# A row-sum kernel whose first load shrinks to 128 neighbouring rows, with a block transpose and two more stores

One core of one Trainium2 chip. The metric is the time of one execution on the device, in microseconds (us), as the median of several runs. All runs quoted are at a granted clock of 1.0. A profiled run has a span of its own, from the first to the last instruction; it is 1.7 to 1.8 us shorter than the time.

## The reference

```python
x = np.random.randn(32, 512, 1024).astype(np.float32)      # 67.11 MB
def reference(x):
    return np.sum(x, axis=-1).astype(np.float32)           # 16384 sums
```

Each of 16384 rows of 4 KB is summed. Nothing is used twice, so the kernel is a stream of loads with sums beside it.

## The kernel before

The rows are taken in 8 groups. In a group each of the 128 partitions holds 16 rows that lie behind one another in memory (64 KB). Three buffers of one group each rotate. The first group comes in two loads, 4 rows and 12 rows a partition; the last group in small pieces, so that little is left to sum after the last byte. Loads are issued from the queue of SyncE (SP). `hold(a, b, why)` lets instruction a wait for b. The start barrier, where the engines wait for each other, stands ahead of the kernel's body; the first load is moved ahead of it.

```python
def issue_first_load_at_entry(nc):          # run on the finished program
    ...                                     # (finds SP's first load in its block: `load`)
        entry = list(main.instructions)
        k = next(k for k, i in enumerate(entry) if isinstance(i, mybir.InstDrain) and i.engine == SP)
        main.instructions = entry[:k] + [load] + entry[k:]     # ahead of the start barrier
...
    x_g = x.flatten_outer_dims().rearrange("(g p j) d -> g p j d", p=P, j=BIG)   # BIG = 16
    def rows_from(j, n):
        return x_g[j // BIG, :, j % BIG : j % BIG + n, :]
    FIRST = 4
...
        for g in range(last):
            t = inpool.tile([P, BIG * dim + 4], fp32)
            if g == 0:
                rows(t, 0, FIRST, 0, 0)            # load on SP, then one reduce on VectorE
                first = sums_of[-1]
                rows(t, FIRST, BIG - FIRST, FIRST, 0)
                continue
            load = rows(t, 0, BIG, g * BIG, BIG // 2 if g == last - 1 else 0)
            if g == 1:
                hold(load, first, "no descriptors of later loads while the first ones start")
...                                                # last group in five pieces
        hold(store(nc.scalar, 0, last), two, "its packets come behind those of the loads")
...
        store(nc.sync, last, last + 1)
```

Of the kernel before, what the change touches and what calls it, by code (L numbers as in the profile page):

```python
# [89 lines left out]
@with_exitstack  # L90
def kernel(
    ctx: ExitStack,
    tc: tile.TileContext,
    x: bass.AP,
    out: bass.AP,
):
    nc = tc.nc
    nc.at_finalize(issue_first_load_at_entry)
    nc.at_finalize(order_waits)
    nc.at_finalize(wait_for_the_store_at_the_clear)  # L100
    fp32 = mybir.dt.float32
    P = 128
    batch, seq, dim = x.shape
    rows = batch * seq
    J = rows // P
    BIG = 16


    x_g = x.flatten_outer_dims().rearrange("(g p j) d -> g p j d", p=P, j=BIG)
    out_v = out.rearrange("b s -> (b s)").rearrange("(g p j) -> p g j", p=P, j=BIG)  # L110

    def rows_from(j, n):
        return x_g[j // BIG, :, j % BIG : j % BIG + n, :]



    last = J // BIG - 1
    FIRST = 4
    pieces = (560, 464)

    with (
        tc.tile_pool(name="in", bufs=3) as inpool,
        tc.tile_pool(name="unread", bufs=4, space=bass.MemoryType.PSUM) as upool,
        tc.tile_pool(name="stage", bufs=1) as stpool,
        tc.manual_schedule(),
    ):
        sums = stpool.tile([P, J], fp32)

        def vec(dst, src):
            return nc.vector.tensor_reduce(  # L130
                out=dst, in_=src, axis=mybir.AxisListType.X, op=mybir.AluOpType.add
            )

        def hold(inst, until, reason):
            tc.add_manual_dep(
                inst.ins,
                until.ins.name,
                mybir.DependencyInfo(mybir.DependencyClass.Sync, mybir.DependencyReason.DATA),
                reason=reason,
            )  # L140

        def halves(dst, src):
            n = src.shape[-1] // 2
            return nc.vector.tensor_tensor_reduce(  # L144
                out=src[:, :n],
                in0=src[:, :n],
                in1=src[:, n:],
                scale=1.0,
                scalar=0.0,
                op0=mybir.AluOpType.add,  # L150
                op1=mybir.AluOpType.add,
                accum_out=dst,
            )

        def act(dst, src, n):
            unread = upool.tile([P, dim], fp32)
            nc.scalar.activation(  # L157
                out=unread[:, :n],
                in_=src,
                func=mybir.ActivationFunctionType.Copy,  # L160
                accum_out=dst,
            )

        sums_of = []

        def rows(t, a, n, j, n_act, pairs=False):
            nv = n - n_act
            block = t[:, a * dim : (a + n) * dim].rearrange("p (n d) -> p n d", d=dim)
            load = nc.sync.dma_start(out=block, in_=rows_from(j, n))  # L169
            if pairs:  # L170
                for q in range(nv):
                    sums_of.append(halves(sums[:, j + q : j + q + 1], block[:, q, :]))
            else:
                sums_of.append(vec(sums[:, j : j + nv], block[:, :nv, :]))
            for q in range(nv, n):
                act(sums[:, j + q : j + q + 1], block[:, q, :], dim)
            return load

        def store(eng, g0, g1):
            return eng.dma_start(  # L180
                out=out_v[:, g0:g1],
                in_=sums[:, g0 * BIG : g1 * BIG].rearrange("p (g j) -> p g j", j=BIG),
            )

        for g in range(last):
            t = inpool.tile([P, BIG * dim + 4], fp32)
            if g == 0:
                rows(t, 0, FIRST, 0, 0)
                first = sums_of[-1]
                rows(t, FIRST, BIG - FIRST, FIRST, 0)  # L190
                continue
            load = rows(t, 0, BIG, g * BIG, BIG // 2 if g == last - 1 else 0)
# [4 lines that stand above are left out]
        j = last * BIG  # L197
        rows(t, 0, 8, j, 4)
        rows(t, 8, 5, j + 8, 2, pairs=True)
        two = rows(t, 13, 2, j + 13, 1, pairs=True)  # L200
        a = BIG - 1



        j += a
        c, width = pieces
        whole = t[:, a * dim + c : BIG * dim + 2]
        nc.vector.memset(whole[:, width + 1 :], 0.0)  # L208
        part = t[:, a * dim : a * dim + c]
        nc.sync.dma_start(out=part, in_=rows_from(j, 1)[:, 0, :c])  # L210
        nc.sync.dma_start(out=whole[:, 1 : width + 1], in_=rows_from(j, 1)[:, 0, c:])
        hold(store(nc.scalar, 0, last), two, "its packets come behind those of the loads")
        halves(whole[:, :1], part)
        halves(sums[:, j : j + 1], whole)
        store(nc.sync, last, last + 1)
# [30 lines left out]
```

## Time and profile before

| | before |
|---|---|
| time, median of 3 runs | 161.77 us (161.68 to 161.86) |
| span of the profiled run | 160.2 us |
| VectorE busy | 120.1 us, 75% |
| loads' queue, share of 16 DMA engines' span | 97.7% |
| first load issued, second load issued | 0.00, 0.78 us |

The DMA engines are the bound and VectorE has slack; the prediction shows how that is read. One more view: the timeline of VectorE in the first 45 us. Columns: start in us, duration in us, engine, line, operation, what it writes and reads, and in brackets how long the engine had been idle and what ended that.

```profile
7.16 4.42 DVE L130 TENSOR_REDUCE sums<-t 128x4 f32<-128x4096 f32 x1 [7.16 <-DMA t<-in_x_dram]
21.68 12.95 DVE L130 TENSOR_REDUCE sums<-t 128x12 f32<-128x12288 f32 x1 [10.10 <-DMA t<-in_x_dram]
41.05 17.22 DVE L130 TENSOR_REDUCE sums<-t 128x16 f32<-128x16384 f32 x1 [6.42 <-DMA t<-in_x_dram]
```

A reduce starts when all 16 DMA engines have landed their parts, so each start here is a clock on the stream: 8.39 MB are in at 21.68, 16.78 MB at 41.05.

### The profile page before, as it was taken

The page shows a single profiled execution, that of the slowest core. Times are in us where ns is not written, and L with a number is a line of the kernel's source. Part 1 is how long each engine was busy: PE and PEld are TensorE (multiplying, and loading weights), DVE is VectorE, ACT ScalarE, POOL GpSimd, SP SyncE. Part 2 cuts the span into 40 slices and gives each one's busy share as a digit, 9 for nine tenths or more (in the row PEclk, how much of TensorE's full clock was granted, in tenths as well). Part 3 has the DMA queues.
Part 4 walks back from the last instruction along what each step waited for, and adds up shares of the span by engine and source line. Part 5 has one row for each costly group of instructions (what it writes and reads, how often), then busy time and mean ns, then how long its engine had stood idle before and what let it go on. Part 6 is the DMA issues. An engine that isn't in the chain of part 4 may idle for free.

```text
span 160.2 us, 125 instructions
## 1 busy us (share of the span) xinstructions
DVE 120.1 (75%) x22; ACT 17.3 (11%) x31; POOL 0.2 (0%) x4
## 2 busy tenths in 40 slices
DVE  0280059960799959999499994999949998597943
ACT  3000000000000000000000000000000000596952
POOL 0000000000000000000000000000000000000000
DMA  7999996996996996996996997998969969999994
GB/s 262 458 466 515 393 523 262 523 523 262 523 523 262 523 523 262 523 523 262 523 491 294 523 458 327 523 409 376 523 262 523 523 262 523 393 393 425 409 379 112
DMA packets 2928, 67.18 MB, mean 419 GB/s; under 512 B 1264, under 2 KB 1392, under 8 KB 1520
## 3 DMA queue, kind: packets, MB, share of 16 engines
q1 hardware_dynamic: 2016, 67.12, 97.7%
q10 hardware_dynamic: 912, 0.06, 0.4%
HBM read 67.11 MB, written 0.07 MB: 419 GB/s over the span
## 4 chain that ended last, share of the span: by engine, by line
DMA 73%; DVE 25%; SPq 1%; issue 0%; DVEq 0%
DMA t<-in_x_dram 73%; DVE sums L130 24%; SPq L169 1%; SPq L210 0%; DVE t L144 0%; DVEq L241 0%
## 5 line engine op out<-in xcount | busy, mean ns | idle before, releaser
L130 DVE TENSOR_REDUCE sums<-t 128x16 f32<-128x16384 f32 (+3 forms) x9 | 116.6, 12953 | 35.5 <-DMA t<-in_x_dram 35.5
L157 ACT ACTIVATE unread<-t 128x1024 f32<-128x1024 f32 x15 | 15.2, 1010 | 139.6 <-DMA t<-in_x_dram 139.6
L144 DVE CUSTOM_DVE_ANT_0 t<-t 128x512 f32<-128x512 f32 (+2 forms) x6 | 3.5, 603 | 2.7 <-DMA t<-in_x_dram 2.6
L157 ACT ACTIVATION_READ_ACCUMULATOR unread<-t 128x1 f32 x15 | 2.8, 186 | 0.0
L157 ACT ACT_TABLE_LOAD x1 | 1.3, 1283 | 0.8 <-PEq L230 0.8
L144 DVE DVE_READ_ACCUMULATOR2_ANT sums<- 128x1 f32 x5 | 0.4, 84 | 0.0
L230 POOL MEMSET const-bfloat16-1.0<- 128x1 bf16 x1 | 0.1, 102 | 0.0
L230 POOL MEMSET const-uint8-127<- 128x1 uint8 x1 | 0.1, 102 | 0.0
L230 POOL MEMSET const-float32-0.0<- 128x1 f32 x1 | 0.1, 99 | 0.2 <-issue 0.2
L230 POOL MEMSET const-float32-1.0<- 128x1 f32 x1 | 0.1, 99 | 0.0
L144 DVE DVE_READ_ACCUMULATOR2_ANT t<- 128x1 f32 x1 | 0.1, 82 | 0.0
L208 DVE MEMSET t<- 128x1 f32 x1 | 0.1, 59 | 0.0
## 6 DMA issues: line engine op xcount, KB each, us to landing
t<-in_x_dram SPq DMA_DIRECT2D x1, 6144.0 KB, 20.9
t<-in_x_dram SPq DMA_DIRECT2D x1, 4096.0 KB, 31.3
t<-in_x_dram SPq DMA_DIRECT2D x1, 2560.0 KB, 37.3
t<-in_x_dram SPq DMA_DIRECT2D x1, 2048.0 KB, 7.1
t<-in_x_dram SPq DMA_DIRECT2D x1, 1024.0 KB, 39.3
t<-in_x_dram SPq DMA_DIRECT2D x1, 280.0 KB, 39.5
t<-in_x_dram SPq DMA_DIRECT2D x1, 232.0 KB, 39.6
t<-in_x_dram SPq DMA_DIRECT2D x6, 40.8
```

The costliest lines, as they stand in the source:

```text
L130: return nc.vector.tensor_reduce(out=dst, in_=src, axis=mybir.AxisListType.X, op=mybir.AluOpType.add)
L144: return nc.vector.tensor_tensor_reduce(out=src[:, :n], in0=src[:, :n], in1=src[:, n:], scale=1.0, scalar=0.0, op0=mybir.AluOpType.add, op ...
L157: nc.scalar.activation(out=unread[:, :n], in_=src, func=mybir.ActivationFunctionType.Copy, accum_out=dst,)
L169: load = nc.sync.dma_start(out=block, in_=rows_from(j, n))
L208: nc.vector.memset(whole[:, width + 1 :], 0.0)
L230: nc = _bacc.Bacc("TRN2", target_bir_lowering=False, num_devices=1)
```

## The change

The first load becomes one row per partition, and the 128 rows are neighbours in memory (0.5 MB in one piece) instead of 4 rows from each partition's 64 KB. VectorE's first sum then starts sooner. Each partition's sum of the first load belongs to a neighbouring output address, so a store straight from the column would be 128 pieces of 4 bytes; a 32x32 block transpose turns it into four rows of 32 sums. The second load has 15 rows per partition. The sums of group 0 no longer fit the common store and get two of their own.

```diff
+    FIRST = 1
+    x_0 = x_g[0].rearrange("p j d -> (p j) d")
+    out_0 = out.rearrange("b s -> (b s)")[: P * BIG]
+    x_first = x_0[: FIRST * P, :].rearrange("(p j) d -> p j d", j=FIRST)
+    x_second = x_0[FIRST * P :, :].rearrange("(p j) d -> p j d", j=BIG - FIRST)
+    SQ = 32
+    out_first = out_0[:P].rearrange("(s c) -> s c", c=SQ)
+    out_second = out_0[FIRST * P :].rearrange("(p j) -> p j", j=BIG - FIRST)
     def rows_from(j, n):
+        if j < BIG:
+            return x_first if j == 0 else x_second
         return x_g[j // BIG, :, j % BIG : j % BIG + n, :]
-    FIRST = 4
...
             if g == 0:
-                rows(t, 0, FIRST, 0, 0)
+                column = stpool.tile([P, SQ], fp32)
+                turned = stpool.tile([P, SQ], fp32)
+                nc.vector.memset(column, 0.0)
+                rows(t, 0, FIRST, 0, 0, sums_to=column)
                 first = sums_of[-1]
+                nc.vector.transpose(out=turned, in_=column)
+                nc.scalar.dma_start(out=out_first, in_=turned[0:P:SQ, :])
                 rows(t, FIRST, BIG - FIRST, FIRST, 0)
...
-        hold(store(nc.scalar, 0, last), two, "its packets come behind those of the loads")
+        hold(store(nc.scalar, 1, last), two, "its packets come behind those of the loads")
+        nc.scalar.dma_start(out=out_second, in_=sums[:, FIRST:BIG])
```

More of the change, by code (lines that the diff above doesn't have):

```diff
@@ L164, with rows @@
         sums_of = []
-        def rows(t, a, n, j, n_act, pairs=False):
+        def rows(t, a, n, j, n_act, pairs=False, sums_to=sums):
             nv = n - n_act
@@ L173, in rows @@
             else:
-                sums_of.append(vec(sums[:, j : j + nv], block[:, :nv, :]))
+                sums_of.append(vec(sums_to[:, j : j + nv], block[:, :nv, :]))
             for q in range(nv, n):
```

## The prediction

> **What bounds the kernel now.** I began with the page's header, its busy shares and its chain of what ended last, because they say whether an engine or the memory sets the end.
>
> ```profile
> span 160.2 us, 125 instructions
> ...
> DVE 120.1 (75%) x22; ACT 17.3 (11%) x31; POOL 0.2 (0%) x4
> ...
> q1 hardware_dynamic: 2016, 67.12, 97.7%
> ...
> DMA 73%; DVE 25%; SPq 1%; issue 0%; DVEq 0%
> ```
>
> VectorE, the busiest engine, idles for a quarter of the span; the loads' queue (q1) keeps all 16 DMA engines busy for 97.7% of it. The chain gives VectorE 25%, which looks as if it mattered. To see whether it does I read the chain in order of time and the timeline of the middle.
>
> ```profile
> 0.00 7.13 DMA t<-in_x_dram
> 7.16 4.43 DVE sums L130
> 11.61 29.43 DMA t<-in_x_dram
> 41.05 17.23 DVE sums L130
> 58.30 40.78 DMA t<-in_x_dram
> ...
> 60.40 17.22 DVE L130 TENSOR_REDUCE sums<-t 128x16 f32<-128x16384 f32 x1 [2.13 <-DMA t<-in_x_dram]
> 79.75 17.22 DVE L130 TENSOR_REDUCE sums<-t 128x16 f32<-128x16384 f32 x1 [2.13 <-DMA t<-in_x_dram]
> 99.10 17.22 DVE L130 TENSOR_REDUCE sums<-t 128x16 f32<-128x16384 f32 x1 [2.13 <-DMA t<-in_x_dram]
> ```
>
> Every reduce waits 2.13 us for its data, so VectorE never holds the stream back. It stands in the chain because a load is issued when a reduce frees its buffer. But look at the load issued at 58.30: it lands 40.78 us later, at 99.08. A load of 16 rows takes 99.10 - 79.75 = 19.35 us to move, so for some 21 us it only stood in the queue behind another one. The chain's VectorE pieces are slack: two loads are always ahead. From load to load 8.39 MB take 19.35 us, 433.5 GB/s. At that rate 67.11 MB take 154.8 us, so only about 5.4 us of the 160.2 are anything else: the start before packets flow, and the tail. The change touches just these two, so I looked at each in small windows and at the tail's issues.
>
> ```profile
> 0.75:1.00 0.25, 0.00 (x0) 0.22 (x1) 0.00 (x0) 1.00 0.00 0
> 1.00:1.25 0.25, 0.00 (x0) 0.25 (x1) 0.00 (x0) 1.00 4.13 918
> ...
> 156.62 0.41 ACTq L180 DMA_DIRECT2D out_dram<-sums  x1
> 158.32 0.35 SPq L180 DMA_DIRECT2D out_dram<-sums  x1
> ...
> out_dram<-sums ACTq DMA_DIRECT2D x1, 56.0 KB, 2.1
> out_dram<-sums SPq DMA_DIRECT2D x1, 8.0 KB, 1.4
> ```
>
> The first packets appear 1.0 us after the first issue. The big store is issued at 156.62 and lands 2.1 us later (158.7); the last store is issued at 158.32 and lands 1.4 us later (159.7). Half a microsecond after that the program ends.
>
> **What the Trainium skill says.** "DMA: Bandwidth & Descriptors", section "Where 436 GB/s comes from", gives 435.2 GB/s as the ceiling of the 16 ports. The trace agrees: 433.5 GB/s from load to load. There is nothing to win inside the stream. The same page, "Why a DMA increments its semaphore by 16 and not by 1", says that a DMA issued from SP or ACT runs on the largest number of engines up to 16 that divides the slowest dimension of both sides. So a store of 4 pieces should run on 4 engines; no DMA of the kernel before has such a shape, so the trace doesn't show it. "VectorE: DVE Perf Modes", section "The perf-mode tier table", has tensor_reduce at one element per cycle only. The trace agrees: 4420 ns for 4096 columns and 17220 for 16384, a slope of 1.04 ns a column and about 0.15 us besides. The same page, "The three transpose paths", says that VectorE transposes within 32x32 blocks and lists 311 ns for 128x128 bf16. That is why the diff reads one row of each of four blocks (partitions 0, 32, 64, 96). No transpose is in the trace before.
>
> **The change part by part.**
>
> First load. It shrinks from 2 MB (16 KB a partition) to 0.5 MB (4 KB a partition); the second grows from 6 MB to 7.5 MB (60 KB a partition). Bytes together, number of loads, and packets (one per partition and load, 128 each) stay. In the packet records a 16 KB packet repeats on its engine every 607 ns and a 48 KB one every 1812 ns, so 27.2 GB/s and some 5 ns fixed. By that 4 KB take 156 ns and 60 KB 2264 ns. One engine handles 8 packets of each load: before 8 x (0.607 + 1.812) = 19.35 us, after 8 x (0.156 + 2.264) = 19.36 us. Equal to 0.01 us.
>
> Can a hole open between the two loads? That is the main danger of a small first load. The second load is issued at 0.78 us (after the start barrier, unchanged). If it needs the same 1.0 to 1.3 us to its first packet as the first one, its packets are ready by 1.8 to 2.1 us. Before, the engines ended their first load between 6.48 and 6.78 us; eight packets at 607 ns are 4.86, so their common delay is 1.6 to 1.9 us. With eight 4 KB packets they would end at 1.6 + 1.25 = 2.9 to 3.2 us. So the second load is there 0.8 us before it is needed. No hole; 0.0 us.
>
> VectorE at the start. The first reduce starts at about 3.2 + 0.4 = 3.6 us instead of 7.16 (before, 0.4 us lay between the last packet and the reduce), and takes 1024 x 1.04 + 0.15 = 1.2 us instead of 4.42. A memset of 128x32 runs before it in idle time, a transpose of 128x32 after it: under 0.3 us as an estimate from the fixed 0.15 us and 32 columns. The second reduce is still started by its data at 21.7 us and takes 15 x 1024 x 1.04 + 0.15 = 16.2 us, ending at 37.8 instead of 34.6. The load that waits for this buffer is then issued 3.2 us later, but data ahead of it in the queue last until 60 us. 0.0 us.
>
> The third load. It is held until the first sum, so it is issued at about 4.8 instead of 11.6 us, behind the second one, whose packets flow by then. The hold was made against descriptors in the first phase; that phase is over. Estimate 0.0 to +0.1 us.
>
> Early store. Four pieces of 128 B, issued by the otherwise idle ScalarE queue near 5 us. The packets of the late store took 8 to 19 ns each; one on each of four engines amid 154 us of stream is at most +0.05 us. It costs an issue of 0.4 us and delays the table load, both 130 us before ScalarE is needed.
>
> Tail. The big store falls from 7 to 6 groups (48 KB) and a second of 7.5 KB follows. Issue 156.62 + 0.41 + a gap of 0.05 puts the second issue at about 157.1. First packets came 0.92 us after the issue of the big store, so the second one's run from 158.0 on, 8 per engine, and land near 158.7: the time at which the one store landed before. The final SP store, issued at 158.32 with packets from 159.16, meets nobody. 0.0 us on the path.
>
> The sum: 0.01 + 0.0 + 0.0 + 0.05 + 0.05 + 0.0, some +0.1 us at most. I take +0.05, thus 161.8 us.
>
> **The rivals.**
>
> A hole at the start. If the second load's packets came later than 3 us, because its descriptors queue behind something or the first small packets don't hide latency, each engine would idle until they come. For: before, the first packet of an engine took 0.83 to 1.47 us instead of 0.61, so the start is not smooth. Against: the 0.8 us of room above. It would make +0.2 to +0.8 us, 162.0 to 162.6.
>
> The tail gets longer. If 60-byte pieces at a pitch of 60 bytes are written slowly, the second store lands after the point at which the end waits for it. SP passes its wait for the big store by 158.9, the end needs the last store at 159.77, and some 0.4 us of barrier steps lie between. So there are about 0.4 us of slack, and only a landing after 159.1 would cost: +0.2 to +0.5 us, up to 162.3. Against: 64-byte packets took 8 to 19 ns.
>
> A gain. Sums start 3.6 us sooner and the tail's big store is an eighth smaller. If VectorE's start were on the path, as the chain's 4.43 us suggests, up to 6.8 us would go (155 us). Against: the stream is at 433.5 GB/s throughout and 154.8 us long whatever VectorE does. A small gain is possible if the many short packets fill the engines more smoothly at the start: -0.1 to -0.3 us.
>
> **Range and chances.** Without a rival it is 161.8. The small gain sets the low end, 161.4; half of the hole or of the tail sets the high end, 162.3. Two per cent are 3.2 us: for a gain that is more than half of all that is not streaming, so 0.01. For a loss a new fault would have to appear, as that 60 KB packets move slower than 64 KB ones, so 0.02. Within 2%: 0.97.
>
> **What would show it.** Right: the first reduce at 3.4 to 3.8 us and 1.2 us long; third load issued before 5.5 us; DMA share near 1 from 1.5 us on; the second reduce starting at 21.6 to 21.9 us and the third at 41.0 to 41.3; reduces still waiting about 2.1 us each; the last store issued at 158.2 to 158.5; the second ScalarE store landing before 159.1. A second reduce later than 22.0 us would mean the hole; an equal last issue with a longer span would mean the tail; loads that come more than 19.4 us apart would mean that the stream itself was disturbed.

## The result and the profile after

| | before | after |
|---|---|---|
| time, median of 6 runs each | 161.81 us (161.68 to 162.53) | 162.85 us (162.37 to 163.33) |
| ratio, 95% interval | | 1.0059 (1.0033 to 1.0084) |
| span of the profiled run | 160.2 us | 161.6 us |

A ratio is the mean time of one kernel's runs over that of the other's of the same rounds, so not quite the ratio of the medians. The change costs 0.6%, and 162.85 lies above the predicted 161.4 to 162.3.

The header and the loads' queue of the page after, then its chain of what ended last in order of time (start, duration, what):

```profile
span 161.6 us, 130 instructions
...
q1 hardware_dynamic: 2016, 67.12, 97.0%
```

```profile
0.00 3.27 DMA t<-in_x_dram
...
3.37 1.23 DVE column L142
...
4.62 38.13 DMA t<-in_x_dram
42.75 0.02 issue
42.77 17.23 DVE sums L142
```

The chain has the same form as before, but the third reduce, the one after 16.78 MB, starts at 42.77 instead of 41.05. VectorE's timeline after shows where that comes from:

```profile
3.37 1.22 DVE L142 TENSOR_REDUCE column<-t 128x1 f32<-128x1024 f32 x1 [2.42 <-DMA t<-in_x_dram]
4.62 0.21 DVE L206 STREAM_TRANSPOSE turned<-column 128x32 f32<-128x32 f32 x1
4.87 1.08 ACTq L207 DMA_DIRECT2D out_dram<-turned  x1
...
23.39 16.15 DVE L142 TENSOR_REDUCE sums<-t 128x15 f32<-128x15360 f32 x1 [18.55 <-DMA t<-in_x_dram]
42.77 17.22 DVE L142 TENSOR_REDUCE sums<-t 128x16 f32<-128x16384 f32 x1 [3.23 <-DMA t<-in_x_dram]
...
158.42 0.55 ACTq L231 DMA_DIRECT2D out_dram<-sums  x1
...
159.62 0.35 SPq L192 DMA_DIRECT2D out_dram<-sums  x1
```

The same 8.39 MB are in at 23.39 instead of 21.68. From there to the next start it is 19.38 us, as before. So 1.71 us are lost by the end of the second load, and no more after it; in the last group some is won back. The issues view says it in one line for each kernel, first before, then after (size, us from issue to landing; both are issued at 0.78 us):

```profile
t<-in_x_dram SPq DMA_DIRECT2D x1, 6144.0 KB, 20.9
```

```profile
t<-in_x_dram SPq DMA_DIRECT2D x1, 7680.0 KB, 22.6
```

To see how, one must go to the single packets. Each engine's packets of a load, and the small completion write behind them, can be told apart in the trace's packet records. This table is computed from them:

| | before | after |
|---|---|---|
| engines end the first load | 6.48 to 6.78 us | 2.46 to 2.92 us |
| first packets of the second load take | 1.815 us each (48 KB), all 16 | 2.27 to 3.34 us (60 KB; 2.27 later on) |
| the five engines that are last begin the second load | at once | at 3.18 to 3.75 us |
| second packets take | 1.815 us | 2.27 to 3.05 us |
| engines end the second load | 20.98 to 21.28 us | 21.40 to 23.04 us |
| spread of the engines there | 0.30 us | 1.64 us |
| last load's last packet ends | 157.44 us | 158.69 us |

After the change the second load starts unevenly. An engine that is behind stays behind: each one works off its own packets at 27 GB/s. The fastest engine has lost 0.4 us by the end of the second load, the slowest 1.8, and a reduce waits for the slowest. Of 1.76 us at the second load 1.24 are left at the last one: the kernel before loses half a microsecond in the last group's pieces (32 KB packets of up to 1.38 us instead of 1.21, 20 KB packets of up to 0.95 instead of 0.76), the changed kernel doesn't. Why is not shown.

### The profile page after: what moved, and what is told of

It is laid out like the page before. It is cut to its first block, busy times and chain, and to the rows that moved or that the text cites. A ratio compares the mean times of both kernels' runs of the same rounds, so it can differ in the third digit from the quotient of the medians.

```text
span 161.6 us, 130 instructions
## 1 busy us (share of the span) xinstructions
DVE 120.3 (74%) x24; ACT 17.3 (11%) x31; POOL 0.2 (0%) x4
## 4 chain that ended last, share of the span: by engine, by line
DMA 75%; DVE 22%; SPq 1%; issue 0%; DVEq 0%
DMA t<-in_x_dram 75%; DVE sums L142 21%; DVE column L142 1%; SPq L181 1%; SPq L228 0%; DVE t L156 0%; DVEq L142 0%; DVEq L260 0%
## 5 line engine op out<-in xcount | busy, mean ns | idle before, releaser
L142 DVE TENSOR_REDUCE sums<-t 128x16 f32<-128x16384 f32 (+3 forms) x8 | 115.4, 14420 | 33.5 <-DMA t<-in_x_dram 33.5
L142 DVE TENSOR_REDUCE column<-t 128x1 f32<-128x1024 f32 x1 | 1.2, 1220 | 2.4 <-DMA t<-in_x_dram 2.4
```

The costliest lines, as they stand in the source:

```text
L142: return nc.vector.tensor_reduce(out=dst, in_=src, axis=mybir.AxisListType.X, op=mybir.AluOpType.add)
```

## The experiments

All are timed in 5 rounds beside the kernel before on the same chip. Four theories were tried first: S, the short first load; N (later P), the neighbouring rows or the second load's pitch; T, the new stores; H, the earlier descriptors of the third load. Two more came later: W, memory that no load touched before; R, the second load isn't ready when the engines come to it. The expectations also use two names. By its use, Y says that the first load's own rows make the start uneven, whatever the second load meets. In the last two runs S seems to mean that the first load's addresses lie close together (0.5 MB), and no longer that it is short.

Two numbers are read from every run's trace. The **lead** is the time from the issue of a load to the end of the load ahead of it on the first engine: how long the load has been under way when the first engine turns to it. The **spread** is the time between the first and the last engine's end of the second load.

**One part at a time.** A small first load with the rows as before:

```diff
# kernel before
-    FIRST = 4
+    FIRST = 1
```

> The kernel before with a first load of one row per partition instead of four, rows as before (4 KB at a pitch of 64 KB), no transpose, no additional stores. Theory S (a short first load leaves the engines without work that hides the start of the second load): as slow as the changed kernel, +0.8 to +1.3 us over the kernel before, second reduce starts 1.3 to 2 us later than 21.7. Theory N (the neighbouring rows, or the second load's pitch of 60 KB, are read slower at the start): within 0.3 us of the kernel before. Theory T (the stores do it): within 0.3 us.

Measured: 162.18 us, ratio 1.0017 (1.0002 to 1.0032); second reduce at 22.18, lead 2.20, spread 0.53 us. The size alone costs some 0.3 us (by the interval 0.5 at most), so S is not the main cause.

Neighbouring rows at the old size, stores in the middle of the kernel:

```diff
# kernel before
+    x_first = x_0[: 4 * P, :].rearrange("(p j) d -> p j d", j=4)
+    x_second = x_0[4 * P :, :].rearrange("(p j) d -> p j d", j=BIG - 4)
...                                    # out_first, out_second and rows_from as in the change
+            if g == 3:
+                st = nc.scalar.dma_start(out=out_first, in_=sums[:, :FIRST])
+                hold(st, sums_of[-1], "in the middle of the kernel")
+                nc.scalar.dma_start(out=out_second, in_=sums[:, FIRST:BIG])
...                                    # the late store on ScalarE begins with the second group
```

> A first load of 2 MB as before, but of 512 neighbouring rows, four per partition; the second load of 12 neighbouring rows per partition; their sums are stored in the middle of the kernel (sixteen-byte and 48-byte pieces, after the fourth group's reduce), so that start and tail have no additional store. Theory S: within 0.3 us of the kernel before, second reduce starts near 21.7. Theory N: +0.5 us or more, second reduce near 23. Theory T: within 0.3 us.

Measured: 162.33 us, ratio 1.0028 (1.0010 to 1.0045). The second load is perfectly even, 1.815 us for each of its packets. The loss lies inside the first load, whose slowest engine ends at 7.44 instead of 6.78 us. So neighbouring rows cost something themselves, but not this way.

The early store moved away from the start, and the third load held back:

```diff
# changed kernel, first of the two
-                nc.scalar.dma_start(out=out_first, in_=turned[0:P:SQ, :])
...
+            if g == 3:
+                st = nc.scalar.dma_start(out=out_first, in_=turned[0:P:SQ, :])
+                hold(st, sums_of[-1], "in the middle of the kernel")
# changed kernel, second of the two
+                idle = stpool.tile([P, 1650], fp32)
+                for _ in range(6):
+                    first = nc.vector.memset(idle, 0.0)
```

> The changed kernel with its four-piece store put off until after the fourth group's reduce (some 80 us). Theory T (the early store's descriptors, whose issue took 1.08 us at 4.9 us, disturb the second load's start): the second reduce back near 21.7 and the time within 0.3 us of the kernel before. Theories S, N and H (the third load's descriptors): no change from the changed kernel, +0.8 to +1.3 us.

Measured: 162.96 us, ratio 1.0068 (1.0041 to 1.0094), as slow as the changed kernel. The early store is not the cause.

> The changed kernel, with memsets on the idle VectorE after the first sum that the third load is held for, so that it is issued at 10 us or later (11.6 in the kernel before) instead of 4.6. Theory H (the descriptors of the third and fourth load come while the second load starts and slow it): half or more of the 1.0 us returns, second reduce at 22.3 or earlier. Theories S, N, T: no change, second reduce near 23.4, +0.8 to +1.3 us over the kernel before.

Measured: 164.02 us, ratio 1.0127 (1.0105 to 1.0149); the third load is issued at 15.9 us, and the packets that start near 5.0 us still take 2.3 to 2.9 us. H falls. That this kernel is another 1.1 us slower was expected by no theory, and stays unexplained.

**The two loads crossed.** On the kernel before with FIRST = 1, only the addresses of the first two loads are changed. Three of these kernels give wrong sums on purpose.

```diff
# kernel before, FIRST = 1; strided: x_g[0, :, :1, :] and x_g[0, :, 1:, :]
     def rows_from(j, n):
+        if j < BIG:
+            return x_first if j == 0 else x_second
# e5: strided first, neighbouring second; e6: neighbouring first, strided second; e7: both neighbouring
# e8 (correct): rows as before, third load held by four memsets
```

> WRONG result on purpose (some rows are summed twice, some never). Loads alone: the first load as in the run with a small first load (4 KB of each 64 KB), the second load as in the changed kernel (60 KB pieces of neighbouring memory from 0.5 MB on). No additional store, no transpose. Theory P (the 60 KB pitch of the second load's pieces collides at its start): slow start, +0.7 us or more, engines apart by over 1 us after the second load. Theory W (a load that starts on memory which no load has touched pays a start cost, hidden only by long packets ahead of it; the strided first load touches every 64 KB block): smooth start, +0.3 us as with the small first load alone, engines apart by under 0.6 us.

Measured: 161.98 us, ratio 1.0003 (0.9986 to 1.0020); lead 2.11, spread 0.63 us.

> WRONG result on purpose. The other cross: the first load of 128 neighbouring rows, the second of 60 KB pieces at a pitch of 64 KB, as before. Theory P: smooth, within 0.4 us of the kernel before. Theory W: slow start, +0.7 us or more, engines apart by over 1 us.

Measured: 163.57 us, ratio 1.0093 (1.0066 to 1.0120); lead 1.79, spread 1.28 us. The cross is clear: the rows of the first load decide, those of the second don't. P falls.

> WRONG result on purpose (sums land in wrong places). The changed kernel's two first loads, without its memset, transpose and two additional stores. If the loads alone cost the time: +0.8 to +1.3 us, like the changed kernel. If the early store's descriptors or the tail's second store have a share of it: +0.5 us or less. The engines' second packets of the second load (5.0 to 7.8 us) near 2.27 us each would say that the early store had slowed them.

Measured: 164.18 us, ratio 1.0137 (1.0119 to 1.0156); lead 1.80, spread 2.39 us; second packets took 2.6 to 3.0 us without any early store. The two loads cost all of the time by themselves. Why they cost twice as much here as in the changed kernel stays open.

> The kernel before with a first load of one row per partition (layout as before), and the third load held by four memsets until 11 to 12 us. If the +0.3 us of the small first load came from the third load's earlier descriptors: within 0.1 us of the kernel before. If from the start of the second load behind short packets: still +0.3 us.

Measured: 162.11 us, ratio 1.0010 (0.9994 to 1.0026). Not told apart from the run without the hold (1.0017).

**Untouched memory or time.** W fitted all of this. So did a theory of time, R, because the neighbouring first load also ends sooner.

```diff
# changed kernel, e9: the first load once more, ahead of the second
+                again = stpool.tile([P, dim], fp32)
+                nc.sync.dma_start(out=again, in_=x_first[:, 0, :])
                 rows(t, FIRST, BIG - FIRST, FIRST, 0)
# changed kernel, e10: 64 bytes of each piece of the second load, ahead of it
+                touch = stpool.tile([P, 16], fp32)
+                nc.sync.dma_start(out=touch, in_=x_second[:, 0, :16])
                 rows(t, FIRST, BIG - FIRST, FIRST, 0)
# kernel before, e11: no split
-                rows(t, 0, FIRST, 0, 0)
-                first = sums_of[-1]
-                rows(t, FIRST, BIG - FIRST, FIRST, 0)
+                idle = stpool.tile([P, 1650], fp32)
+                for _ in range(6):
+                    first = nc.vector.memset(idle, 0.0)
+                rows(t, 0, BIG, 0, 0)
```

> The changed kernel, with its first load issued a second time (into a buffer that nobody reads) ahead of the second load: 16 packets of 4 KB per engine instead of 8, 1.25 us of more transfer. Theory R (the engines come to the second load before its descriptors are ready, as the short first load ends too soon): they come 1.25 us later, the second load starts smoothly, and its first and second packets last 2.27 us. Theory W (start cost of memory not touched before; the packets ahead touch only the first 0.5 MB and are short): the second load starts as unevenly as in the changed kernel, engines apart by over 1 us after it, and the kernel is some 1.2 us slower than the changed one, 164 us.

Measured: 164.21 us, ratio 1.0141 (1.0117 to 1.0166). Without the 1.25 us of added transfer that is the changed kernel's loss again. But what suffers is now the repeated load: it has a lead of 1.65 us, and its engines end it 1.17 us apart (4.02 to 5.19). It reads memory that has just been read, so W doesn't explain it. My expectation for R missed: the second load was not smooth either (0.94 us apart). I then read R anew: whatever load is next, here the repeated one, is hit. The run with both loads ahead of the barrier tests that reading.

> The changed kernel, with a load of 64 bytes from the start of each of the second load's 128 pieces (8 KB in all, into a buffer that nobody reads) between the first and the second load. Theory W: the cost is paid by these small packets, several at once, so the second load starts smoothly and half or more of the loss returns: 162.4 us or less, engines apart by under 0.8 us. Theory R: the second load is issued 0.4 us later, so nothing is better, 162.9 us or more.

Measured: 163.63 us, ratio 1.0093 (1.0075 to 1.0111); lead of the touching load 1.74, of the second load behind it 1.73, spread 2.10 us. Eight of the 128 packets of 64 bytes came only at 3.9 us, the others by 3.12.

> The kernel before without any split of its first group: 16 rows per partition in one load, the second one held until six memsets have passed (some 12 us). If short packets at the start expose a start cost and VectorE has slack, this is at least as fast as the kernel before: 161.5 to 161.9 us. If the split served something at the start, 162 us or more.

Measured: 162.11 us, ratio 1.0006 (0.9990 to 1.0023). The split of the first group serves nothing that shows, and its absence gains nothing.

> The changed kernel once more, word for word, beside the runs of this call. 162.4 to 163.3 us as in its first runs if the kernel repeats; as slow as 164 us if the difference between it and the loads alone (164.2 us) is only where and when it runs.

Measured: 162.90 us, ratio 1.0055 (1.0025 to 1.0086), runs from 162.13 to 163.83. The changed kernel repeats, with a wide spread of its runs.

**W against what the first load does.**

```diff
# changed kernel, e13: touch of the second load's pieces as the very first transfer, first load behind it,
#                      both ahead of the start barrier (moved as in e17 below)
+                touch = stpool.tile([P, 16], fp32)
+                nc.sync.dma_start(out=touch, in_=x_second[:, 0, :16])
                 rows(t, 0, FIRST, 0, 0, sums_to=column)
# kernel before, FIRST = 1, e14: first load twice, as in e9
# kernel before, e15 (FIRST = 1) and e16 (FIRST = 4), wrong sums on purpose:
     def rows_from(j, n):
+        if j == 0:
+            return x_g[4, :, :n, :]
```

> The changed kernel, with a load of 64 bytes from the start of each of the second load's pieces issued as the very first transfer, the first load right behind it (both ahead of the start barrier). Theory W: the second load, 1 to 2 us later, starts smoothly; engines apart by under 0.7 us after it; about 162.0 to 162.4 us. Theory Y: still rough, engines apart by over 1 us, 162.9 us or more.

Measured: 162.52 us, ratio 1.0054 (1.0025 to 1.0084); runs of 162.1 to 162.6 and two near 163.45. The profiled run is one of the fast ones: lead 1.82, spread 0.61 us. In between.

> The kernel with a small strided first load, that load issued twice: the control of the neighbouring load issued twice. 1.25 us of transfer more than the small first load alone (162.2): 163.4 us. If the dip after 2.5 us, which the repeated neighbouring load showed, belongs to the time and not to the rows, it shows here too and the repeated load's last packet ends 1.8 us or more after the first load's; theories W and Y say 1.3 us.

Measured: 163.85 us, ratio 1.0120 (1.0098 to 1.0141); lead of the repeated load 2.04, which ends 4.16 to 4.84, spread after the second load 0.54 us. There is no dip; 0.4 us more than my sum of 1.25 and 0.3.

> WRONG result on purpose. As the small strided first load, but it reads the first 4 KB of each 64 KB of the fifth group, so the second load (first group) meets memory that no load has touched. The first load's shape, packets and pitch are the same. Theory W: rough, +0.7 us or more, engines apart by over 1 us after the second load. Theory Y: smooth, +0.0 to +0.4 us, engines apart by under 0.6 us.

Measured: 162.17 us, ratio 1.0015 (1.0001 to 1.0029); lead 2.04, spread 0.46 us. The second load met untouched memory and was as even as in the run with the small first load alone. W falls.

> WRONG result on purpose. The same with the first load of the kernel before, 16 KB of each 64 KB, read from the fifth group. If long packets ahead hide the cost of untouched memory (as the 2 MB of neighbouring rows suggest): second load smooth, its packets 1815 ns, within 0.3 us of the kernel before. If only the touching helped the kernel before: rough, +0.5 us or more.

Measured: 161.75 us, ratio 0.9996 (0.9978 to 1.0013); second load's packets 1.815 us. The first load of the kernel before doesn't owe its smooth sequel to having touched those rows.

**The lead alone.** The last two runs.

```diff
# changed kernel, e17: the second load, too, ahead of the start barrier
         entry = list(main.instructions)
+        at = next(
+            k for k, i in enumerate(insts) if isinstance(i, mybir.InstDMACopy) and i.engine == SP
+        )
+        load = [load, insts.pop(at)]
...
+        block.instructions = insts
-        main.instructions = entry[:k] + [load] + entry[k:]
+        main.instructions = entry[:k] + load + entry[k:]
...
# changed kernel, e18: as e13, but touching the first load's own rows
+                nc.sync.dma_start(out=touch, in_=x_first[:, 0, :16])
```

> The changed kernel, with its second load, too, issued ahead of the start barrier, right behind the first (at 0.4 instead of 0.78 us). Theory R: engines come to it 2.1 to 2.5 us after its issue, as behind a strided first load: smooth, engines apart by under 0.7 us after it, 162.3 us or less. Theory S: still rough, engines apart by 1 us or more, 162.7 us or more.

Measured: 161.93 us, ratio 0.9992 (0.9973 to 1.0011). The whole loss is gone. Nothing but the issue of the second load has moved, from 0.78 to 0.41 us; the engines end the first load as before, from 2.46 us on, so the lead is 2.05 instead of 1.68, and the spread is 0.51 us. VectorE's timeline of this kernel:

```profile
3.44 1.22 DVE L148 TENSOR_REDUCE column<-t 128x1 f32<-128x1024 f32 x1 [2.04 <-DMA t<-in_x_dram]
4.69 0.21 DVE L212 STREAM_TRANSPOSE turned<-column 128x32 f32<-128x32 f32 x1
21.68 16.15 DVE L148 TENSOR_REDUCE sums<-t 128x15 f32<-128x15360 f32 x1 [16.77 <-DMA t<-in_x_dram]
41.04 17.22 DVE L148 TENSOR_REDUCE sums<-t 128x16 f32<-128x16384 f32 x1 [3.20 <-DMA t<-in_x_dram]
...
158.23 0.35 SPq L198 DMA_DIRECT2D out_dram<-sums  x1
```

The second reduce starts at 21.68 and the third at 41.04, as in the kernel before (21.68 and 41.05), with all of the change's other parts still in place. SP's first two issues, merged into one row from the start of the first to the end of the second, in the changed kernel and in this one (the second starts at 0.78 and at 0.41):

```profile
0.00 1.11 SPq L181 DMA_DIRECT2D t<-in_x_dram  x2
```

```profile
0.00 0.84 SPq L187 DMA_DIRECT2D t<-in_x_dram  x2
```

> The changed kernel, with a load of 64 bytes from each of the first load's own 128 rows as the very first transfer, the first load behind it ahead of the barrier: packets and delays of the spread touch at entry (162.5 us, engines 0.6 us apart), but within 0.5 MB. Theory S: rough, engines apart by 1 us or more, 163.0 us or more. If the delay and not the spread smoothed the start: as with the spread touch.

Measured: 163.48 us, ratio 1.0094 (1.0065 to 1.0123), runs from 162.44 to 164.24; the profiled run is the fastest: lead 1.79, spread 0.78 us. Slow at a lead below 2 us, as R would have it; whether the spread touch at entry did better (1.0054) by its place or by chance is not settled, as the intervals overlap.

Sorted by lead, all kernels whose first group has a small first load (for repeated or touching loads the lead is that of the load right behind the first one, the touch at entry not counted):

| kernel | lead, us | spread, us | ratio |
|---|---|---|---|
| neighbouring load twice | 1.65 | 0.94 (1.17 after the repeated load) | 1.0141, of which 1.25 us added transfer |
| changed kernel | 1.68 | 1.64 | 1.0059 |
| touch between the loads | 1.74 | 2.10 | 1.0093 |
| changed kernel again | 1.77 | 1.78 | 1.0055 |
| neighbours, then strided | 1.79 | 1.28 | 1.0093 |
| touch of own rows at entry | 1.79 | 0.78, fastest run | 1.0094 |
| store later | 1.80 | 1.23 | 1.0068 |
| loads of the changed kernel alone | 1.80 | 2.39 | 1.0137 |
| touch of the pieces at entry | 1.82 | 0.61, a fast run | 1.0054 |
| third load later | 1.85 | 2.77 | 1.0127 |
| strided elsewhere | 2.04 | 0.46 | 1.0015 |
| strided load twice | 2.04 | 0.54 | 1.0120, of which 1.25 us added transfer |
| both at entry | 2.05 | 0.51 | 0.9992 |
| strided, then neighbours | 2.11 | 0.63 | 1.0003 |
| strided, third load later | 2.13 | 0.48 | 1.0010 |
| strided | 2.20 | 0.53 | 1.0017 |

Up to 1.85 us of lead a kernel loses 0.5% or more; from 2.04 us on at most 0.2%, but for the strided load twice, which loses 0.4% beyond its additional transfer (1.95 us less 1.25).

Two limits. Each lead comes from the one profiled run of its kernel, and the two touches at entry show fast runs (162.13 and 162.44 us) that were nearly even at 1.82 and 1.79 us: a short lead goes with the loss in most runs, not in all. And the neighbouring first loads all have leads up to 1.85 us but for one run, the strided ones 2.04 or more. Only the run with both loads at entry parts the two. A strided first load with its second load issued later was not run, so a short lead is shown to cost time behind neighbouring rows only.

## Why the prediction was wrong

The prediction's verdict, within 2%, was right, but its time was not. It said +0.05 us, the chip +1.0.

**The step that failed** is the question "Can a hole open between the two loads?", answered by "So the second load is there 0.8 us before it is needed. No hole; 0.0 us." Two terms of that 0.8 us were wrong.

- Readiness. The step took the 1.0 to 1.3 us from a load's issue to its first packets for the time that it needs. The first packets are not the full stream. In the kernel before, the packet records give some 220 GB/s between 1.25 and 2.25 us, 332 at 2.25 to 2.5 and 430 only from 3.0 us on. The prediction's range left out one engine of the kernel before: 15 first packets start at 1.00 to 1.29 us, the sixteenth at 1.79 (it took 0.74 us, below the 0.83 to 1.47 that the prediction gives). With the lead as the variable, loads were even from 2.04 us after their issue and mostly uneven up to 1.85. By that estimate engines could come to the second load, issued at 0.78, only from some 2.6 to 2.8 us on, not from 1.8 to 2.1. That a load's slow first rate is the reason is argued, not shown.
- Arrival. The step had the engines end the first load at 2.9 to 3.2 us. That is right for strided rows (2.97 to 3.25 in the run with the small first load), but neighbouring rows are through at 2.46 to 2.92, and the first reduce began at 3.37, ahead of the 3.4 to 3.8 given as a sign. The step took the start delay of one address pattern for that of another.

Together the room was some -0.4 to -0.2 us (2.46 - 0.78, less 2.04 or 1.85) instead of +0.8. The run that issues the second load 0.37 us sooner, and changes nothing else, returns all of the loss. That shows the cause: the second load's issue comes too late for a first load that ends this early. The rival "A hole at the start" named it and gave the right sign to look for ("A second reduce later than 22.0 us would mean the hole": it came at 23.39). But I had sized it at 0.2 to 0.8 us, as a plain gap. The loss was larger than the gap, because an uneven start leaves engines up to 1.8 us behind, and the stream ends with the slowest.

Two slips beside that changed nothing: the large store shrinks by a seventh (56 to 48 KB), not an eighth, and the rival gain of 6.8 us comes neither from the chain's 4.43 us nor from the 5.4 us that are not streaming.

**What held.** VectorE's early start is worth nothing: the sum starts 3.8 us sooner and no later reduce is moved by it. The first sum took 1.22 us as said, the transpose 0.21 within its estimate of 0.3. The early store uses four engines: the scalar queue's packets went from 912 to 936, and 768 + 16 for the large store, 128 + 16 for the second and 4 + 4 for the early one make 936. Moving it away changed nothing. The tail held: the second scalar store was issued 0.44 us after the large one (0.46 predicted), and the final store 0.43 us after the start of the last sum (159.62 against 159.19), as before (158.32 against 157.88). The third load's earlier issue was predicted at 0.0 to +0.1; holding it back didn't help. The early store's issue took 1.08 us instead of 0.4, which nobody waits for.

**What stays open.** What happens inside a load's first 2 us (the descriptors, their fetching, the memory) is not visible in these traces. With nearly the same lead, kernels lost between 0.5% and 1.4%, some steadily (164.05 to 164.32 us for the two loads alone), some with widely spread runs (162.13 to 163.83 for the changed kernel again); no run explains the difference. Neighbouring rows in a 2 MB first load cost 0.3% though the lead was 5.8 us. And in the slow kernels the packets of 5 to 8 us, too, take up to 3 us, on engines that had started in time.

## What to carry to other kernels

In this stream of loads the second load had to be issued some 2 us before the engines came to it. A short first load leaves less time for that, and a start barrier stood between the two issues. The short first load saved nothing in any run, not even with the second load issued right behind it. The first packet (1.0 us after the issue) is too early a measure of when a load can follow another without a gap. No version beat the kernel before beyond noise: the changed kernel with both loads ahead of the barrier only equals it, so the kernel before is to be kept.

## What the Trainium skill lacked or had wrong

- "DMA: Bandwidth & Descriptors", section "Specifications", gives a first-byte latency of about 0.6 us for transfers issued from SP or ACT. It doesn't say from where it counts. In these runs the first load's first packets came 1.0 us after the start of its issue, thus about 0.6 us after the end of the issue, which took 0.38 us: counted so, page and trace agree. Some 420 GB/s were reached only 2.25 us (small strided first load) to 2.75 us (kernel before) after the issue. The page has no figure for that, nor for the lead that the load behind needs (up to 1.85 us mostly uneven, from 2.04 even).
- No page says that engines which start a load unevenly stay apart: in the changed kernel they are 1.64 us apart after the second load and still 1.64 us (157.05 to 158.69) after the last one, 136 us later.
- "VectorE: DVE Perf Modes", section "The three transpose paths", has one size only (311 ns for 128x128 bf16); 128x32 in fp32 took 211 ns.
- No page has the issue time of a store that reads every 32nd partition: 1.08 us for four pieces of 128 bytes, at 4.9 us as well as at 97.7 us (the run with the store later), against 0.40 and 0.55 us for the changed kernel's 128-partition stores from the same queue.
